# GLA values of two heads in one product of 512 columns, with the last gates and the first head's weight loads placed elsewhere

## The chip, the cores and the metric

The kernel runs on one core of a Trainium2 chip. The metric is the device time of one execution in microseconds (us), from the start of the program to its end. A core has five engines with their own instruction streams: PE (TensorE, the matmuls, with PEld for the weight loads), DVE (VectorE), ACT (ScalarE), POOL (GpSimd) and SP (SyncE), which issues most of the DMAs. Each engine executes its stream in order. Streams wait for one another through semaphores.

## The reference

One layer of a decoder on 2048 prompt tokens and 64 sample tokens (8 sequences of 8), with model width 1024. An input projection feeds two branches; the branches are merged by sigmoid gates, projected once more and normalized. The part that the change touches is the second branch, gated linear attention (GLA), with 4 heads of 128 keys and 256 values.

```python
z = jnp.einsum('btd,dn->btn', x, w_in)
q, k, v, g_att, gq, gk, gv, g_gla, g_lr, r_att, r_gla = jnp.split(z, SPLIT_POINTS, axis=-1)
...
def step(S, xs):                       # GLA, one chunk of tokens
    qc, kc, vc, gc = xs
    b = jnp.cumsum(gc, axis=1)
    b_last = b[:, -1]
    qt = qc * jnp.exp(b)
    kt = kc * jnp.exp(-b)
    kend = kc * jnp.exp(b_last[:, None] - b)
    o_inter = jnp.einsum('bthk,bhkv->bthv', qt, S)
    A = jnp.where(causal, jnp.einsum('bthk,bshk->bhts', qt, kt), 0.0)
    o_intra = jnp.einsum('bhts,bshv->bthv', A, vc)
    S = jnp.exp(b_last)[..., None] * S + jnp.einsum('bshk,bshv->bhkv', kend, vc)
    return S, o_inter + o_intra
...
o_gla = o_gla * lax.rsqrt(jnp.mean(jnp.square(o_gla), -1, keepdims=True) + EPS) * gla_norm_w
h_att = jnp.einsum('bta,ad->btd', o_att * jax.nn.silu(g_att), w_pa)
h_gla = jnp.einsum('btv,vd->btd', o_gla * jax.nn.silu(g_gla), w_pg)
merged = jax.nn.sigmoid(r_att) * h_att + jax.nn.sigmoid(r_gla) * h_gla
y = jnp.einsum('btd,de->bte', merged, w_o)
```

## The kernel before

Every dense product is made of three matmuls on values split in a high and a low part (fp32r): high by high, high by low, low by high. ACT casts the high part (L122) and DVE subtracts it from the value for the low part (L123). `proj` (L210 to L212) has weights stationary and tokens as columns; `proj_t` (L223 to L225) has the tokens stationary and the weights as columns, so its output has tokens on partitions.

The program has four stages. Attention runs from 0 to about 408 us: the 2112 tokens go in six chunks of 384, 384, 384, 384, 256 and 320 columns (`CHUNKS`), and in each the projections alternate with pieces of softmax work. GLA follows until about 1061 us: a loop over the 4 heads, in each the same six chunks. Then come four merge passes (L1268 to L1270), which use a Strassen-like recombination of blocks, and at last the output projection w_o with 512 columns per matmul (also L223 to L225).

In one GLA chunk the order on PE is written out by hand: the decay input (`gla_z`), values v for each block of 128 tokens (256 columns of one head), then k, q and two gate products g0 and g1. The recurrence of a chunk, the chain, runs through `at` and `tick`: `at(n, f)` puts f in a side list, and each `tick()` between products emits what is due. Its steps are `gla_a` (k by q for one block, masked by L763, and the key transpose), `gla_b` (output and state update, with the state split for the next block) and `gla_c` (the output's transpose, multiplied into the gate tile `sg` at L813). The chain of one chunk runs during the products of the next. In the last chunk of head 3 it runs during its own gates (`mid` puts a tick inside a product), and the sample tokens follow (`samp_a`, `samp_b`).

The order on the other engines comes from the framework's scheduler, which emits each engine's work as its operands become due; their streams are then fixed. Activations x are stored split in DRAM (`xs_d`) and loaded per chunk on SP; the gate input `gin` is loaded on POOL's queue. Finished gate tiles are stored to `ug_d` on SP, in the last chunk of head 3 on POOL. Three kinds of side work are threaded in: weight loads (`wload`, tile wst, cast to wh at L122 and wl at L123, up to a limit set by `wcap`), combinations of blocks for the merge passes (`combine_load` at L886, sums at L892 to L895, stores at L897), and in the last attention chunk the first head's weights. In that chunk `step` calls `wload` after every product, and `keys` writes kT (L611) after the key splits (L368 to L374).

Of the kernel before, what the change touches and what calls it, by code (L numbers as in the profile page):

```python
# [12 lines left out]
F32 = mybir.dt.float32  # L13
# [8 lines left out]
P = 128  # L22
# [28 lines left out]
def xwide(c):  # L51


    return 2 * CHUNKS[c][1] + (NS if c == len(CHUNKS) - 1 else 0)
# [3 lines left out]
def kernel(ctx, tc, io):  # L58
# [13 lines left out]
    def pd():  # L72
        return psd.tile([P, 512], F32, tag="pd", name="pd")
# [4 lines left out]
    def wtile(dt=F32, name="w"):  # L78
        return sb.tile([P, D], dt, tag="w", name=name, bufs=25)
# [16 lines left out]
    ac_d = dram.tile([4, P, MS, 2, MT], F32, name="ac_d")  # L96
    uc_d = dram.tile([4, P, MS, KT // 2, MT], F32, name="uc_d")
    xs_d = [dram.tile([4, P, 2 * xwide(c)], F32, name=f"xs{c}_d") for c in range(len(CHUNKS))]
    gl_d = dram.tile([96, NT], F32, name="gl_d")
    bs_d = dram.tile([NH, P, LB], F32, name="bs_d")  # L100

# [3 lines left out]
    def at(d, fn):  # L105

        while len(side) <= d:
            side.append([])
        side[d].append(fn)
# [34 lines left out]
    def wget():  # L144
        if not wready:
            wload()
        return wready.popleft()
# [173 lines left out]
    def setup1():  # L321


        oh, rbh, rbl, ssel, scol = (st1[n] for n in ("oh", "rbh", "rbl", "ssel", "scol"))
        for h in range(0, NH, 2):
            brow = wtile(name="brow")[:, :2 * LB].rearrange("p (h j) -> p h j", h=2)
            for j in range(2):
                bps = pa()
                mm(bps[:, :LB], rbh[:, h + j], oh, start=True, stop=False)
                mm(bps[:, :LB], rbl[:, h + j], oh, start=False, stop=True)  # L330
                if j:
# [3 lines left out]
            nc.sync.dma_start(bs_d[h:h + 2].rearrange("h q j -> q h j"), brow)  # L335
# [225 lines left out]
    def wcap(n):  # L561
        wseq[1] = n
# [18 lines left out]
    for c, (t0, T) in enumerate(CHUNKS):  # L581
# [13 lines left out]
        def step(ps_use, w=None):  # L595
            if w is not None:
                ps = pd()
                proj(ps[:, :T], w, x, T)
                ps_use(ps[:, :T])
            if last:  # L600
                wload()
            tick()

        if last:
            gin = gate_in(0, 0)

# [95 lines left out]
    def rot(key):  # L702
        r = R[key][cnt[key] % len(R[key])]
        cnt[key] += 1
        return r
# [63 lines left out]

    def gla_norm(B, key, o, n):  # L770

        on = rot("on")
        sq = small([P, 1], "sq")
        nc.scalar.activation(on[:n], o, AF.Square, scale=1.0 / 16, accum_out=sq[:n])  # L774
        nc.gpsimd.tensor_scalar(sq[:n], sq[:n], EPS, None, op0=ALU.add)  # L775
        nc.gpsimd.tensor_tensor(sq[:n], sq[:n], mhalf[:n], ALU.pow)
        nc.scalar.mul(on[:n], o, sq[:n])
        B["on", key] = on
# [35 lines left out]

    def gla_store(B):
        for m in range(2):
            (nc.gpsimd if B["last"] and B["h"] == GH - 1 else nc.sync).dma_start(
                ug_d[B["h"]][:, m, B["t0"]:B["t0"] + B["T"]], B["sg"][m][:, :B["T"]])


# [78 lines left out]
    def chain(B):  # L899

        last, nt = B["last"], B["nt"]
        if B["h"] == 0 and B["t0"] == 0:
            rings()
        short = nt == 2 and not last
        for i in range(nt):
            at(i, lambda B=B, i=i: gla_a(B, i))
            at((3, 5)[i] if short else i + 2, lambda B=B, i=i: gla_b(B, i))
            at((6, 7)[i] if short else i + 4, lambda B=B, i=i: gla_c(B, i, P, i * P))
        if last:
            at(nt + 2, lambda B=B: (nc.gpsimd if B["h"] == GH - 1 else nc.sync).dma_start(  # L910
                io["o_sp"][B["h"]], R["S"][sstate[B["h"]]]))
            at(nt - 1, lambda B=B: samp_a(B))
            at(nt + 1, lambda B=B: samp_b(B, 0))
            at(nt + 2, lambda B=B: samp_b(B, 4))
            o = nt + 4 if B["h"] == GH - 1 else nt + 5
            at(o, lambda B=B: gla_c(B, "s", NS, B["Tp"]))
            at(o, lambda B=B: gla_store(B))
        else:
            at(7 if short else 6, lambda B=B: gla_store(B))

    for h in range(GH):
        W2 = {}
        wcap(16 + 6 * h)
        for c, (t0, T) in enumerate(CHUNKS):
            last = c == len(CHUNKS) - 1
            Tp = T - (NS if last else 0)
            nt = Tp // P
            if c == len(CHUNKS) - 3:
                wcap(min(22 + 6 * h, 34))
            B = dict(h=h, t0=t0, T=T, Tp=Tp, nt=nt, last=last, wgk=R["wgk"], gin=gin, gv=[], sg=[])  # L930

            def wt2(*key):
                if c == 0:
                    W2[key] = wget()
                return W2[key]

            gla_z(B)
# [7 lines left out]
            wv = [wt2("v", 0), wt2("v", 1)]  # L945
            for i in range((T + P - 1) // P):
                n = min(P, T - i * P)
                ps = pd()
                if n == P:
                    proj_t(ps[:, :HV], x, i * P, n, wv, HV)  # L950
                    v = ps[:, :HV]
                else:
                    v = unit(name="vs")[:n, :HV]
                    proj_s(ps[:, :HV], v, x, i * P, wv, HV)
                    nc.vector.tensor_tensor(v, v, ps[:n, :HV], ALU.add)
                if i % 2 == 0:
                    gvt = wtile(F32R, "gv").rearrange("p (a b v) -> p a b v", a=2, b=2)
                gh, gl = gvt[:, i % 2, 0], gvt[:, i % 2, 1]
                split(gh[:n], gl[:n], v)
                if n == NS:  # L960
                    nc.scalar.copy(gh[NS:], v)
                    nc.vector.tensor_tensor(gl[NS:], v, gh[:NS].bitcast(F32), ALU.subtract)
                B["gv"].append((gh, gl))
                if last and i < 2:
                    wload()
                tick()
            end = last and h == GH - 1
            if not end:
                xn = tiles(load_x((c + 1) % len(CHUNKS)))
            ps = pd()  # L970
            proj(ps[:, :T], wt2("k"), x, T)
            gla_k(B, ps[:, :T])
            combine()
            if len(CHUNKS) - 4 < c < len(CHUNKS) - 1:
                wload()
            tick()
            if not last:
                gin = gate_in(h, c + 1)
            elif h + 1 < GH:
                gin = gate_in(h + 1, 0)  # L980
            ps = pd()
            proj(ps[:, :T], wt2("q"), x, T)
            gla_q(B, ps[:, :T])
            tick()
            combine()
            if end:
                chain(B)
            for m in range(2):
                sg = unit(name="sg")
                B["sg"].append(sg)  # L990
                w = wt2("g", m)
                ps = pd()
                proj(ps[:, :T], w, x, T, mid=end)
                gate(sg, ps[:, :T], T)
                if len(CHUNKS) - 4 < c < len(CHUNKS) - 1 and m == 1:
                    wload()
                tick()
            if not end:
                chain(B)
            x = xn  # L1000


# [384 lines left out]
def _layout(i):  # L1387
# [20 lines left out]
    wo = a["w_o"][0]  # L1408
    t = [cm(k), cm(v)] + [cm(heads(q, g)) for g in range(G)] + [cm(heads(ga, g)) for g in range(G)]
    for h in range(GH):  # L1410
        vh = gv[:, h * HV:(h + 1) * HV].reshape(2, 4, P, HV).transpose(0, 2, 1, 3).reshape(2, P, D)
        t += [vh[0], vh[1], cm(gk[:, h * HK:(h + 1) * HK]), cm(gq[:, h * HK:(h + 1) * HK])]
        t += [cm(gg[:, h * HV + m * P:h * HV + (m + 1) * P]) for m in range(2)]
    t_o = [rows(wo[:, nh * 512:(nh + 1) * 512], k0) for nh in range(2) for k0 in range(0, KT, 2)]

    def blocks(m):
# [58 lines left out]
```

## Time and profile before

| what | value |
|---|---|
| median of 3 executions | 1863.12 us (1858.07, 1863.60, 1863.12) |
| profiled execution | 1860.13 us, span 1858.4 us |
| mean granted TensorE clock in it | 0.989 |
| busy in the span | DVE 1196.7 us, ACT 770.0 us, POOL 391.2 us |
| DMA traffic | 368.98 MB, mean 199 GB/s |

The page gives busy time by engine, the span in 40 slices, DMA queues, the chain of work that ended last, and the costliest groups of instructions, each with the idle time before it and what ended that. "L210 PE MATMUL pd<-x,wh 128*128 128x384" is line 210, writing pd from the operands x and wh. A bracket such as [7.89 <-ACT kT L611] after an instruction says that its engine stood idle 7.89 us, and that ACT's write of kT at line 611 ended that. A matmul's own duration contains the pipeline; the pace of a stream is read from start to start.

### The profile page before, as it was taken

The page shows a single profiled execution, that of the slowest core. Times are in us where ns is not written, and L with a number is a line of the kernel's source. Part 1 is how long each engine was busy: PE and PEld are TensorE (multiplying, and loading weights), DVE is VectorE, ACT ScalarE, POOL GpSimd, SP SyncE. Part 2 cuts the span into 40 slices and gives each one's busy share as a digit, 9 for nine tenths or more (in the row PEclk, how much of TensorE's full clock was granted, in tenths as well). Part 3 has the DMA queues.
Part 4 walks back from the last instruction along what each step waited for, and adds up shares of the span by engine and source line. Part 5 has one row for each costly group of instructions (what it writes and reads, how often), then busy time and mean ns, then how long its engine had stood idle before and what let it go on. Part 6 is the DMA issues. An engine that isn't in the chain of part 4 may idle for free.

```text
span 1858.4 us, 31579 instructions
## 1 busy us (share of the span) xinstructions
PE 1809.5 (97%) x11683; PEld 1721.9 (93%) x11683; DVE 1196.7 (64%) x2470; ACT 770.0 (41%) x1735; POOL 391.2 (21%) x511
## 2 busy tenths in 40 slices
PE   7999999999999999999999989999999999989997
PEld 6998998889999999999999989999999999977886
DVE  5676777556665565566555559658657566966655
ACT  4444444443553454445444443445454543211110
POOL 2400000201011011011010124420355253631111
PEclk8999999999999999999999989999999999999999
DMA  7621234355565555745655089858887967895531
GB/s 263 234 81 63 74 107 162 121 181 191 195 223 177 211 213 177 256 145 191 220 204 177 29 262 322 277 192 284 278 319 261 307 217 245 283 300 188 161 114 40
DMA packets 188858, 368.98 MB, mean 199 GB/s; under 512 B 19981, under 2 KB 135141, under 8 KB 188688
## 3 DMA queue, kind: packets, MB, share of 16 engines
q1 hardware_dynamic: 181936, 357.82, 56.4%
q0 software_dynamic: 5616, 7.58, 1.4%
q8 instruction: 92, 1.51, 0.3%
q10 hardware_dynamic: 1152, 1.57, 0.3%
q14 instruction: 62, 0.51, 0.1%
HBM read 264.17 MB, written 103.70 MB: 198 GB/s over the span
## 4 chain that ended last, share of the span: by engine, by line
PE 86%; DMA 6%; DVE 4%; issue 1%; ACT 1%; POOL 1%; SPq 0%; DVEq 0%; POOLq 0%; ACTq 0%
PE pd L210 11%; PE pd L211 10%; PE pd L212 10%; PE pa L1269 8%; PE pa L1268 8%; PE pa L1270 8%; PE pd L225 6%; PE pd L223 6%; PE pd L224 6%; DMA wst<-wt 2%; DMA cs<-tt_d 2%; PE pa L449 1%; PE pa L434 1%; PE pa L783 1%; PE pa L784 1%
## 5 line engine op out<-in xcount | busy, mean ns | idle before, releaser
L210 PE MATMUL pd<-x,wh 128*128 128x384 f32 (+2 forms) x1248 | 411.1, 329 | 13.2 <-ACT kT L611 7.9
L212 PE MATMUL pd<-x,wl 128*128 128x384 f32 (+2 forms) x1248 | 404.7, 324 | 1.1 <-DVE wl L123 1.1
L211 PE MATMUL pd<-x,wh 128*128 128x384 f32 (+2 forms) x1248 | 405.2, 325 | 0.0
L1269 PE MATMUL pa<-xl,wh 128*128 128x352 f32 x1176 | 380.4, 323 | 8.6 <-DVE xl L123 8.0
L1268 PE MATMUL pa<-xh,wh 128*128 128x352 f32 x1176 | 382.1, 325 | 6.7 <-ACT wh L122 4.4
L1270 PE MATMUL pa<-xh,wl 128*128 128x352 f32 x1176 | 378.9, 322 | 0.0
L210 PEld LDWEIGHTS pd<-x,wh 128*128 128x128 f32 x1248 | 237.7, 190 | 24.0 <-issue 8.9
L212 PEld LDWEIGHTS pd<-x,wl 128*128 128x128 f32 x1248 | 237.4, 190 | 1.7 <-DVE wl L123 1.7
L211 PEld LDWEIGHTS pd<-x,wh 128*128 128x128 f32 x1248 | 237.8, 191 | 1.3 <-DVE x L123 1.2
L1269 PEld LDWEIGHTS pa<-xl,wh 128*128 128x128 f32 x1176 | 222.9, 190 | 12.0 <-DVE xl L123 11.9
L1268 PEld LDWEIGHTS pa<-xh,wh 128*128 128x128 f32 x1176 | 222.2, 189 | 8.6 <-ACT wh L122 5.0
L1270 PEld LDWEIGHTS pa<-xh,wl 128*128 128x128 f32 x1176 | 222.2, 189 | 0.0
L123 DVE TENSOR_TENSOR xl<-xs,xh 128x1408 fp32r<-128x1408 f32 x63 | 111.3, 1766 | 71.0 <-ACT xh L122 70.8
L223 PE MATMUL pd<-wh,x 128*128 128x256 f32 x512 | 147.9, 289 | 0.0
L224 PE MATMUL pd<-wh,x 128*128 128x256 f32 x512 | 144.7, 283 | 0.0
L225 PE MATMUL pd<-wl,x 128*128 128x256 f32 x512 | 144.7, 283 | 0.0
L775 POOL TENSOR_SCALAR sq<-sq 128x1 f32<-128x1 f32 (+1 forms) x68 | 18.6, 274 | 566.1 <-ACT ring L774 566.0
L122 ACT CAST xh<-xs 128x1408 fp32r<-128x1408 f32 x63 | 86.5, 1373 | 106.8 <-PE pa L1270 83.9
L225 PE MATMUL pd<-wol,x 128*128 128x512 f32 x256 | 101.6, 397 | 0.5 <-DVE wol L123 0.5
L123 DVE TENSOR_TENSOR wl<-ws,wh 128x512 fp32r<-128x512 f32 (+1 forms) x112 | 86.9, 787 | 23.2 <-ACT wh L122 22.6
L223 PE MATMUL pd<-woh,x 128*128 128x512 f32 x256 | 101.6, 397 | 0.0
L224 PE MATMUL pd<-woh,x 128*128 128x512 f32 x256 | 101.5, 396 | 0.0
(317 smaller groups left out, 3455.6 us busy)
## 6 DMA issues: line engine op xcount, KB each, us to landing
x<-xs_d SPq DMA_DIRECT2D x64, 768.0 KB, 6.4
wst<-wt SPq DMA_DIRECT2D x33, 512.0 KB, 3.8
xs<-xc_d SPq DMA_DIRECT2D x24, 704.0 KB, 5.7
cs<-tt_d SPq DMA_DIRECT2D x48, 352.0 KB, 4.9
xs<-xT SPq DMA_DIRECT2D x18, 704.0 KB, 6.5
xs_d<-x SPq DMA_DIRECT2D x16, 768.0 KB, 5.3
x<-xs_d SPq DMA_DIRECT2D x16, 704.0 KB, 5.9
ws<-w_ra SPq DMA_DIRECT2D x36, 256.0 KB, 4.6
```

What stands on the lines that cost most here:

```text
L122: pin["a"] = nc.scalar.copy(dst_h, src)
L123: i = eng.tensor_tensor(dst_l, src, dst_h.bitcast(F32), ALU.subtract)
L210: mm(ps, hi[:, s], xh[:, :T], start=(k == 0), stop=False)
L211: mm(ps, hi[:, s], xl[:, :T], start=False, stop=False)
L212: mm(ps, lo[:, s], xh[:, :T], start=False, stop=(k == n - 1))
L223: mm(ps, xh[:, xs], hi, start=(k == 0), stop=False)
L224: mm(ps, xl[:, xs], hi, start=False, stop=False)
L225: mm(ps, xh[:, xs], lo, start=False, stop=(k == KT - 1))
L775: nc.gpsimd.tensor_scalar(sq[:n], sq[:n], EPS, None, op0=ALU.add)
L1268: mm(ps, wh[:, ks], xh[:, ts], start=(k == 0), stop=False)
L1269: mm(ps, wh[:, ks], xl[:, ts], start=False, stop=False)
L1270: mm(ps, wl[:, ks], xh[:, ts], start=False, stop=(k == q.kh - 1))
```

## The change

In even heads the value product covers the head and the next one: `values` uses four weight tiles of 512 columns, and the odd head's half, split, is stored to DRAM (`v_d`). The odd head loads it back (`load_v`). In odd heads the gates come first, with a tick in their middle, then k and q; the chain of the chunk before is shifted by one tick. At the start of k in each chunk, x, gin and (for odd heads) the values of the next chunk are requested (`ahead`). Combine sums run one per chunk from the second chunk on in tiles of their own (`stile`), and one more in two chunks of odd heads. In head 3, chunk 4 emits no gates: its normalized outputs stay in a tile `keep`, and after the last chunk's gates come the two gate products of chunk 4, its `gla_c` steps, and its store, on POOL. In the last attention chunk `wload` is called from the fourth step on. The bias rows of the setup (`brow`) are produced four heads at a time.

```diff
@@ setup
-        for h in range(0, NH, 2):
-            brow = wtile(name="brow")[:, :2 * LB].rearrange("p (h j) -> p h j", h=2)
-            for j in range(2):
+        for h in range(0, NH, 4):
+            brow = xslot(F32, "brow").rearrange("p (h j) -> p h j", h=4)
+            for j in range(4):
...
@@ attention, step
-            if last:
+            steps[0] += 1
+            if last and steps[0] > 3:
                 wload()
...
@@ gla_norm, gla_store
-        on = rot("on")
+        on = B["keep"][:, key * HV:(key + 1) * HV] if "keep" in B else rot("on")
...
-            (nc.gpsimd if B["last"] and B["h"] == GH - 1 else nc.sync).dma_start(
+            (nc.gpsimd if B["h"] == GH - 1 and B["c"] >= LAST - 1 else nc.sync).dma_start(
...
+    def values(B, i):
+        n = min(P, B["T"] - i * P)
+        ps = pd()
+        if n == P:
+            proj_t(ps, x, i * P, n, wv, 512)
+            v = ps
...
+        for j, t in enumerate(B["gvt"]):
+            gh, gl = t[:, i % 2, 0], t[:, i % 2, 1]
+            vj = v[:n, j * HV:(j + 1) * HV]
+            split(gh[:n], gl[:n], vj)
...
+            elif i % 2 or (i + 1) * P >= B["T"]:
+                m = (i % 2 + 1) * 512
+                nc.sync.dma_start(v_d[B["h"] // 2][B["c"]][i // 2, :, :m],
+                                  t.rearrange("p a b v -> p (a b v)")[:, :m].bitcast(F32))
...
+    def load_v(h, c):
...
+            t = wtile(F32R, "gv")
+            nc.sync.dma_start(t[:, :m * 512].bitcast(F32), v_d[h // 2][c][i // 2, :, :m * 512])
...
-            sums = [combine_load(lambda n: wtile(name=n)) for _ in range(2 if c in (1, 2, 3) else 0)]
+            sums = [combine_load(stile)] if c else []
+            if odd and c in (1, 2):
+                sums.append(combine_load(lambda n: wtile(name=n)))
...
+            xn, gin, gvn = ahead()
+            if odd and not end:
...
+                for m in range(2):
+                    gates(B, x, m, True)
...
+            if h == GH - 1 and LAST - 2 <= c < LAST:
+                Bn = chunk(h, c + 1, gin, gvn)
+            dense(B, x, wt2("k"), gla_k, odd)
...
+            if end and not last:
+                B["keep"] = wtile(name="keep")
+                chain(B, 1, late=True)
+                Bg, xg = B, x
+            elif end:
                 chain(B)
+                for m in range(2):
+                    gates(B, x, m, True)
+                for m in range(2):
+                    gates(Bg, xg, m, True)
+                for i in range(Bg["nt"]):
+                    gla_c(Bg, i, P, i * P)
+                drain()
+                gla_store(Bg)
```

Three places in the streams. The first is ACT in the last attention chunk, before the change; pT is the copy of the transposed probabilities, wst the loaded weights and wh their high part, kd the key splits.

```order
L418 ACTIVATE s,sm<-s,nm 128x256 x4
L420 ACTIVATE es<-es 128x4
L122 CAST wh<-wst 128x1024 x2
L438 COPY pT<-pa 128x512
L122 CAST wh<-wst 128x1024
L368 CAST kd_3454<-pd 64x256
L369 CAST kd_3455<-pd 64x256
L373 CAST kd_3454<-pd 64x256
L374 CAST kd_3455<-pd 64x256
L611 COPY kT<-pd 128x320
```

After the change two of the three weight casts are gone from there (the lines below 600 shift by one, the kT line by three).

```order
L419 ACTIVATE s,sm<-s,nm 128x256 x4
L421 ACTIVATE es<-es 128x4
L439 COPY pT<-pa 128x512
L123 CAST wh<-wst 128x1024
L369 CAST kd_3462<-pd 64x256
L370 CAST kd_3463<-pd 64x256
L374 CAST kd_3462<-pd 64x256
L375 CAST kd_3463<-pd 64x256
L614 COPY kT<-pd 128x320
```

The second place is DVE at the end of head 3, where a sum of blocks (x) stands beside the chain (aper is the masked k by q, ak its split, ring the state) and the key products (em, ek). Before:

```order
L763 COPY_PREDICATED aper_170<-cmask,pa 128x128
L123 TENSOR_TENSOR st<-ring,st 128x256
L123 TENSOR_TENSOR ak<-aper_170,ak 128x128
L123 TENSOR_TENSOR ak<-pa,ak 128x128
L892 TENSOR_TENSOR x_11393<-x_11393,x_11392 128x352
L893 TENSOR_TENSOR x_11392<-x_11392 128x352
L894 TENSOR_TENSOR x_11392<-x_11392,x_11393 128x352
L895 TENSOR_TENSOR x_11393<-x_11392,x_11393 128x352
L748 TENSOR_TENSOR em<-pd,em 128x384
```

And after, in head 3's chunk 4:

```order
L895 TENSOR_TENSOR x_11084<-x_11084,x_11083 128x352
L896 TENSOR_TENSOR x_11083<-x_11083 128x352
L751 TENSOR_TENSOR em<-pd,em 128x256
L742 COPY e_11123<-gb 128x2
L745 COPY e_11125<-gb 128x8
L751 TENSOR_TENSOR ek<-pd,ek 128x256
L897 TENSOR_TENSOR x_11083<-x_11083,x_11084 128x352
L766 COPY_PREDICATED aper_180<-cmask,pa 128x128
L898 TENSOR_TENSOR x_11084<-x_11083,x_11084 128x352
L124 TENSOR_TENSOR ak<-aper_180,ak 128x128
L124 TENSOR_TENSOR ak<-pa,ak 128x128
```

The sum now stands ahead of the mask and the splits. Its loads stand on SP (after) behind the store of the sum before and an x load between them:

```order
L195 DMA x<-xs_d 128x1408
L900 DMA uc_d<-x_10826 128x2x352
L900 DMA uc_d<-x_10827 128x2x352
L195 DMA x<-xs_d 128x1408
L889 DMA x_11083<-ug_d 128x704
L889 DMA x_11084<-ug_d 128x704
L195 DMA x<-xs_d 128x1408 x2
```

The third place is the end of GLA. On SP before, the last stores of gate tiles (chunk 4 is 128x256) stand ahead of the first loads of the merge passes, xc and ws:

```order
L817 DMA ug_d<-sg 128x384 x2
L817 DMA ug_d<-sg 128x256 x2
L1073 DMA xc<-ua_d 128x2x352
L1042 DMA ws<-w_pa 128x256 x4
```

After, chunk 4's stores have left SP:

```order
L848 DMA S_11480<-state 128x4x256
L848 DMA S_11482<-state 128x4x256
L820 DMA ug_d<-sg 128x384 x2
L1143 DMA xc<-ua_d 128x2x352
L1112 DMA ws<-w_pa 128x256 x4
```

They are on POOL now, behind those of the last chunk; the xc load takes memory that the gate tiles held, and waits for these stores:

```order
L874 DMA o_ss<-S_11480 128x4x256
L778 TENSOR_SCALAR sq<-sq 64x1
L779 TENSOR_TENSOR sq<-sq,mhalf 64x1
L874 DMA o_ss<-S_11482 128x4x256
L820 DMA ug_d<-sg 128x320 x2
L820 DMA ug_d<-sg 128x256 x2
```

More of the change, by code (lines that the diff above doesn't have):

```diff
@@ L98 @@
     xs_d = [dram.tile([4, P, 2 * xwide(c)], F32, name=f"xs{c}_d") for c in range(len(CHUNKS))]
+    v_d = [[dram.tile([2, P, D], F32, name=f"v{p}{c}_d") for c in range(len(CHUNKS))] for p in range(GH // 2)]
     gl_d = dram.tile([96, NT], F32, name="gl_d")
@@ L330, in setup1 @@
                 mm(bps[:, :LB], rbl[:, h + j], oh, start=False, stop=True)
-                if j:
+                if j % 2:
                     nc.vector.tensor_copy(brow[:, j], bps[:, :LB])
@@ L334, in setup1 @@
                     nc.scalar.copy(brow[:, j], bps[:, :LB])
-            nc.sync.dma_start(bs_d[h:h + 2].rearrange("h q j -> q h j"), brow)
+            nc.sync.dma_start(bs_d[h:h + 4].rearrange("h q j -> q h j"), brow)
         sps = pa()
@@ L599, in step @@
                 ps_use(ps[:, :T])
-            if last:
+            steps[0] += 1
+            if last and steps[0] > 3:
                 wload()
             tick()
+        steps = [0]
         if last:
@@ L897, in combine_do, with chain @@
             nc.sync.dma_start(dst[n_:n_ + 2].rearrange("n p t -> p n t"), x_.rearrange("p (n t) -> p n t", n=2))
-    def chain(B):
+    def chain(B, o=0, late=False):
         last, nt = B["last"], B["nt"]
@@ L903, in chain @@
             rings()
-        short = nt == 2 and not last
+        short = nt == 2 and not last and o == 0
+        end = last and B["h"] == GH - 1
         for i in range(nt):
-            at(i, lambda B=B, i=i: gla_a(B, i))
-            at((3, 5)[i] if short else i + 2, lambda B=B, i=i: gla_b(B, i))
-            at((6, 7)[i] if short else i + 4, lambda B=B, i=i: gla_c(B, i, P, i * P))
+            at(o + i, lambda B=B, i=i: gla_a(B, i))
+            at((3, 5)[i] if short else o + i + 2, lambda B=B, i=i: gla_b(B, i))
+            if not late:
+                at((6, 7)[i] if short else o + i + 4, lambda B=B, i=i: gla_c(B, i, P, i * P))
@@ L909, in chain @@
         if last:
-            at(nt + 2, lambda B=B: (nc.gpsimd if B["h"] == GH - 1 else nc.sync).dma_start(
+            at(o + nt + 2, lambda B=B: (nc.gpsimd if end else nc.sync).dma_start(
                 io["o_sp"][B["h"]], R["S"][sstate[B["h"]]]))
[L912 to L916, printed above, removed]
@@ L917, in chain @@
-            at(o, lambda B=B: gla_store(B))
-        else:
-            at(7 if short else 6, lambda B=B: gla_store(B))
+            at(o + nt - 1, lambda B=B: samp_a(B))
+            at(o + nt + 1, lambda B=B: samp_b(B, 0))
+            at(o + nt + 2, lambda B=B: samp_b(B, 4))
+            at(o + nt + 5, lambda B=B: gla_c(B, "s", NS, B["Tp"]))
+            at(o + nt + 5, lambda B=B: gla_store(B))
+        elif not late:
+            at(7 if short else o + nt + 4 if o else 6, lambda B=B: gla_store(B))
@@ new lines, in values @@
+    def values(B, i):
[4 more added lines that the diff above has]
+            v = ps
+        else:
+            v = wtile(name="vs")[:n, :512]
+            proj_s(ps, v, x, i * P, wv, 512)
+            nc.vector.tensor_tensor(v, v, ps[:n], ALU.add)
+        if i % 2 == 0:
+            B["gvt"] = [wtile(F32R, nm).rearrange("p (a b v) -> p a b v", a=2, b=2) for nm in ("gv", "gvo")]
+        for j, t in enumerate(B["gvt"]):
+            gh, gl = t[:, i % 2, 0], t[:, i % 2, 1]
+            vj = v[:n, j * HV:(j + 1) * HV]
+            split(gh[:n], gl[:n], vj)
+            if n == NS:
+                nc.scalar.copy(gh[NS:], vj)
+                nc.vector.tensor_tensor(gl[NS:], vj, gh[:NS].bitcast(F32), ALU.subtract)
+            if j == 0:
+                B["gv"].append((gh, gl))
+            elif i % 2 or (i + 1) * P >= B["T"]:
+                m = (i % 2 + 1) * 512
+                nc.sync.dma_start(v_d[B["h"] // 2][B["c"]][i // 2, :, :m],
+                                  t.rearrange("p a b v -> p (a b v)")[:, :m].bitcast(F32))
@@ new lines, in load_v, with chunk @@
+    def load_v(h, c):
+        out = []
+        n = (CHUNKS[c][1] + P - 1) // P
+        for i in range(0, n, 2):
+            m = min(2, n - i)
+            t = wtile(F32R, "gv")
+            nc.sync.dma_start(t[:, :m * 512].bitcast(F32), v_d[h // 2][c][i // 2, :, :m * 512])
+            t = t.rearrange("p (a b v) -> p a b v", a=2, b=2)
+            out += [(t[:, j, 0], t[:, j, 1]) for j in range(m)]
+        return out
+    LAST = len(CHUNKS) - 1
+    def chunk(h, c, gin, gv):
+        t0, T = CHUNKS[c]
+        last = c == LAST
+        Tp = T - (NS if last else 0)
+        B = dict(h=h, c=c, t0=t0, T=T, Tp=Tp, nt=Tp // P, last=last, wgk=R["wgk"], gin=gin, gv=gv, sg=[])
+        gla_z(B)
+        return B
@@ L921, with dense, gates, wt2 @@
+    def dense(B, x, w, use, mid):
+        ps = pd()
+        proj(ps[:, :B["T"]], w, x, B["T"], mid=mid)
+        use(B, ps[:, :B["T"]])
+    def gates(B, x, m, mid):
+        sg = unit(name="sg")
+        B["sg"].append(sg)
+        dense(B, x, wt2("g", m), lambda B, ps: gate(sg, ps, B["T"]), mid)
+        tick()
     for h in range(GH):
         W2 = {}
[L923 to L937, printed above, removed]
-            sums = [combine_load(lambda n: wtile(name=n)) for _ in range(2 if c in (1, 2, 3) else 0)]
+        odd = h % 2
+        def wt2(*key):
+            if key not in W2:
+                W2[key] = wget()
+            return W2[key]
+        for c in range(len(CHUNKS)):
+            last = c == LAST
+            end = h == GH - 1 and c >= LAST - 1
+            if not end:
+                B = chunk(h, c, gin, gvn if odd else [])
+            else:
+                B = Bn
+            sums = [combine_load(stile)] if c else []
+            if odd and c in (1, 2):
+                sums.append(combine_load(lambda n: wtile(name=n)))
@@ L943, in combine @@
                         combine_do(*sums.pop(0), nc.vector)
[L945 to L964, printed above, removed]
-                    wload()
-                tick()
@@ L967, with ahead @@
[L967 to L972, printed above, removed]
+            def ahead():
+                nh, nx = (h, c + 1) if not last else (h + 1, 0)
+                if nh == GH:
+                    return None, None, None
+                return tiles(load_x(nx)), gate_in(nh, nx), load_v(nh, nx) if nh % 2 else []
+            if not odd:
+                wv = [wt2("v", i) for i in range(4)]
+                if c == 0:
+                    wcap(wseq[0] + 2)
+                for i in range((B["T"] + P - 1) // P):
+                    values(B, i)
+                    if c == 0:
+                        wload()
+                    tick()
+                if last:
+                    wcap(wseq[0] + 4)
+                    wload(2)
@@ L973 @@
+            xn, gin, gvn = ahead()
+            if odd and not end:
+                if h < GH - 1 and c == 2:
+                    wcap(wseq[0] + 6)
+                for m in range(2):
+                    gates(B, x, m, True)
+                    if last:
+                        wload()
+                if 1 < c:
+                    wload()
+            if h == GH - 1 and LAST - 2 <= c < LAST:
+                Bn = chunk(h, c + 1, gin, gvn)
+            dense(B, x, wt2("k"), gla_k, odd)
             combine()
-            if len(CHUNKS) - 4 < c < len(CHUNKS) - 1:
+            if not odd and last:
@@ L975 @@
                 wload()
             tick()
[L977 to L983, printed above, removed]
+            dense(B, x, wt2("q"), gla_q, odd)
+            if not odd and last:
+                wload()
             tick()
             combine()
-            if end:
-                chain(B)
[L988 to L997, printed above, removed]
@@ L998 @@
-            if not end:
-                chain(B)
+            if end and not last:
[3 more added lines that the diff above has]
+            elif end:
+                chain(B)
+                for m in range(2):
[6 more added lines that the diff above has]
+                gla_store(Bg)
+            else:
+                if not odd:
+                    for m in range(2):
+                        gates(B, x, m, False)
+                chain(B, 1 if (h if not last else h + 1) % 2 else 0)
@@ L1410, in _layout @@
     for h in range(GH):
-        vh = gv[:, h * HV:(h + 1) * HV].reshape(2, 4, P, HV).transpose(0, 2, 1, 3).reshape(2, P, D)
-        t += [vh[0], vh[1], cm(gk[:, h * HK:(h + 1) * HK]), cm(gq[:, h * HK:(h + 1) * HK])]
-        t += [cm(gg[:, h * HV + m * P:h * HV + (m + 1) * P]) for m in range(2)]
+        kq = [cm(gk[:, h * HK:(h + 1) * HK]), cm(gq[:, h * HK:(h + 1) * HK])]
+        gs = [cm(gg[:, h * HV + m * P:h * HV + (m + 1) * P]) for m in range(2)]
+        t += gs + kq if h % 2 else [rows(gv[:, h * HV:(h + 2) * HV], k0) for k0 in range(0, KT, 2)] + kq + gs
     t_o = [rows(wo[:, nh * 512:(nh + 1) * 512], k0) for nh in range(2) for k0 in range(0, KT, 2)]
```

## The prediction

> **What bounds the kernel now.** I read the page's busy shares first.
>
> ```profile
> span 1858.4 us, 31579 instructions
> PE 1809.5 (97%) x11683; PEld 1721.9 (93%) x11683; DVE 1196.7 (64%) x2470; ACT 770.0 (41%) x1735; POOL 391.2 (21%) x511
> PE   7999999999999999999999989999999999989997
> ```
>
> TensorE is busy 97% of the span, so only about 49 us are without matmul work, and the 40 slices put them at the start, at slice 23, near slice 36 and at the end. Next comes the list of what PE waited for.
>
> ```profile
> PE pa L1269 <- DVE xl L123: 8.0, 5, 2.1
> PE pd L210 <- ACT kT L611: 7.9, 1, 7.9
> PE pa L1268 <- ACT wh L122: 4.4, 2, 4.1
> ```
>
> One stall of 7.9 us (kT, the end of attention) and several at the start of the merge passes stand out. Then the stages, by windows (columns: PE, PEld, DVE, ACT, POOL busy, granted clock, DMA share, GB/s).
>
> ```profile
> 408.00:1061.00 653.00, 653.00 (x4747) 646.43 (x4745) 384.75 (x1016) 304.31 (x756) 72.79 (x160) 1.00 0.54 189
> 1300.00:1480.00 180.00, 180.00 (x1135) 180.00 (x1134) 114.24 (x151) 86.02 (x136) 74.92 (x57) 1.00 0.83 290
> 610.00:615.00 5.00, 5.00 (x45) 5.00 (x44) 3.58 (x9) 3.23 (x7) 0.00 (x0) 1.00 1.03 410
> ```
>
> The GLA loop, 408 to 1061, is PE from end to end at full clock. Its time is its matmul time, and there is slack everywhere else: DVE 59%, ACT 47%, DMA 54%. Two things follow. The change can gain there only by fewer or shorter matmul steps, and it can lose there as soon as something else, now hidden, arrives late. All sums are made against the profiled execution, 1860.13 us (span 1858.4); the median of three runs is 1863.12, so that execution is 3.0 us on the fast side. A measurement of this kernel tells about 0.3%, 5.6 us, from no change.
>
> **The 512 columns.** The removed matmuls are the values' 256-column ones, three lines of 512 each; the 512-column kind exists already, in the last stage.
>
> ```profile
> L223 PE MATMUL pd<-wh,x 128*128 128x256 f32 x512 | 147.9, 289 | 0.0
> ```
> ```profile
> 639.88 0.28 PE L225 MATMUL pd<-wl,x 128*128 128x256 f32 x1
> 640.00 0.28 PE L223 MATMUL pd<-wh,x 128*128 128x256 f32 x1
> ...
> 1700.23 0.40 PE L223 MATMUL pd<-woh,x 128*128 128x512 f32 x1
> 1700.47 0.39 PE L224 MATMUL pd<-woh,x 128*128 128x512 f32 x1
> ```
>
> A row's own duration (0.28, 0.40) includes the pipeline; what counts is start to start: 0.120 us at 256 columns, and 0.234 at 512 (ten starts from 1699.76 to 1701.87). 1536 x 0.120 = 184.3 us become 768 x 0.234 = 179.7: **-4.6 us**. Both ends: nothing, if the weight load (0.19 us a piece) were already the pace at either width, and -6. The weight loads halve too, but they overlap. The rows measured stand in for the new ones exactly, so I take -4.6. By the Trainium skill's TensorE: Matmul & The Clock Gate, section Back-to-back issue gap, an isolated matmul takes N/2.4 + 2.5 ns, so a pair of 256 costs only about 2.5 ns more than one of 512 and the sum here would be an estimated -2 us. The trace has 6 ns per pair; the rows decide.
>
> **The first head's weight loads, later.** Before, ACT casts weights in the last attention chunk amid the work that PE waits for.
>
> ```profile
> 320.80 0.58 ACT L438 COPY pT<-pa 128x512 f32<-128x512 f32 x1
> 323.58 1.05 ACT L122 CAST wh<-wst 128x1024 fp32r<-128x1024 f32 x1 [2.21 <-DMA wst<-wt]
> 324.54 0.36 ACT L368 CAST kd<-pd 64x256 fp32r<-64x256 f32 x1
> 327.58 0.36 ACT L373 CAST kd<-pd 64x256 fp32r<-64x256 f32 x1 [2.30 <-DVE kl L372]
> 328.36 0.42 ACT L611 COPY kT<-pd 128x320 f32<-128x320 f32 x1
> ```
> ```profile
> 319.92 1.04 PE L434 MATMUL pa<-ident,s 128*128 128x128 f32 x8
> 328.84 0.64 PE L210 MATMUL pd<-x,wh 128*128 128x320 f32 x1 [7.89 <-ACT kT L611]
> ```
>
> PE ends its transposes at 320.96 and waits for kT until 328.84. ACT could go on at 321.38, but the next cast in its order has no data until 323.58. The new order has one cast there, of weights loaded long before, and then the same kd, kd, kd, kd, kT. So the 2.21 us of DMA wait goes; the cast (1.05), the kd casts and the wait for kl on DVE stay: these are late next. DVE's wl split behind the late cast moves up with it. kT then ends near 326.5 instead of 328.8: **-2.3 us**. Bounds: 0 (kl sets the time regardless) and -7.9 (everything gone). I stay near the 2.21, because that is the only piece whose cause is removed. The loads moved behind step 4 fall in a stretch where PE has products to do.
>
> **Odd heads: a new order, and values read back.** Odd heads do no value products; their values come from DRAM. The work that DVE, ACT and the queues do per chunk shrinks little, but a chunk of 384 columns falls from about 30 us of PE to about 21 us. Hence the density rises: my count of each chunk's DVE operations at their durations gives 0.78 to 0.91 of PE's time in odd heads, against 0.66 at most before. A DVE with that little slack serves its queue in order, and late. Two places come out with no cover, from the order and these rows:
>
> ```profile
> L892 DVE TENSOR_TENSOR x<-x,x 128x352 f32<-128x352 f32 x24 | 12.4, 517 | 0.1
> L748 DVE TENSOR_TENSOR em<-pd,em 128x384 f32<-128x384 f32 x16 | 8.8, 552 | 7.1 <-PE pd L212 7.1
> L763 DVE COPY_PREDICATED aper<-cmask,pa 128x128 f32<-128x128 uint32 x64 | 18.9, 296 | 4.7 <-PE pa L761 2.7
> ```
> ```profile
> x<-xs_d SPq DMA_DIRECT2D x64, 768.0 KB, 6.4
> ...
> x<-ug_d SPq DMA_DIRECT2D x12, 352.0 KB, 5.4
> uc_d<-x SPq DMA_DIRECT2D x12, 352.0 KB, 2.7
> xc<-ac_d SPq DMA_DIRECT2D x12, 352.0 KB, 4.4
> ```
>
> First, **the end of head 3**. The combine sums (L892 to L895 before, L895 to L898 after) now have two buffers of their own. The next sum's load waits for the previous sum's store: 0.4 to issue, 2.7 to land, 0.8 for two issues, 5.4 to land = 9.3 us. In the new order that store stands on SP behind an x load that waits for PE to finish a product, and the sum's four operations stand on DVE ahead of the masks (L763) and splits of the next chain step. Counted from the release of the x load to the splits: 9.3 + 4 x 0.52 + about 1.3 for the masks, multiplications and splits between = 12.7 us, and PE has 10.3 us of work to do before it needs them: 2.4 us of stall. The next sum, built the same way, costs a further 1.5. **+4.0 us**; from 0 (loads land in 3 us) to +8 (both in full, 2 x 4).
>
> Second, **the last chunk of head 1**: q's product takes the PSUM bank of k's, which is freed by two multiplications (L748, about 0.5 each at 320 columns) standing behind two sums of 0.52 and smaller work: 1.0 + 0.8 = **+1.8 us**, from 0 to +3. Gates-first elsewhere, the gate inputs and x loaded at a chunk's start: I cost them at nothing, since x is issued 19 us or more before its use in head 1 and lands in about 6. Where that cover is gone (the last chunk of head 3, 11 us ahead) it just fits. The setup's brow in fours: the same PE work and the same order, 0 within 0.5.
>
> The extra traffic is 17.5 MB, most of it in heads 1 and 3. By my count head 1 moves 40.8 MB in 120.7 us of PE work, 338 GB/s. 290 GB/s took a share of 0.83, so the whole would be 349; 5 us ran at 410. It fits barely, chunk 1 of head 1 above it. **+1.5 us**, from 0 to +8: the worst chunk asks 374 against 349, 21 us x 0.07.
>
> **The tail.** Before, the chain's end runs bare on PE:
>
> ```profile
> 1062.20 0.34 ACT th L245
> 1062.56 0.49 DVE sg L246
> ...
> 1072.22 0.55 POOL ug_d L817
> 1072.77 3.04 DMA ug_d<-sg
> 1075.84 0.35 issue
> 1076.27 2.18 DMA ws<-w_pa
> 1078.48 0.41 ACT wh L122
> ```
> ```profile
> 1062.87 0.38 PE L782 MATMUL pa<-st,qih 128*128 128x256 f32 x1 [0.89 <-ACT st L122]
> ...
> 1070.10 0.70 PE L810 MATMUL pa<-ident,ring 128*128 128x128 f32 x4 [1.01 <-ACT ring L777]
> 1071.07 0.43 PE L1268 MATMUL pa<-xh,wh 128*128 128x352 f32 x1 [0.27 <-ACT wh L122]
> ...
> 1078.93 0.66 PE L1268 MATMUL pa<-xh,wh 128*128 128x352 f32 x1 [4.13 <-ACT wh L122]
> ...
> 1082.62 0.35 PE L1268 MATMUL pa<-xh,wh 128*128 128x352 f32 x1
> ```
>
> From 1071.07 to 1082.62 there are 18 matmuls of 0.160 at full speed, 2.9 us, in 11.55: 8.7 lost, of which about 1.6 is a half clock after the gap (0.29 start to start). With the ring wait (1.2), the gap before 1071.07 (0.5) and the st waits (1.5): 11.9 lost. The change covers the ring wait. But in the new order the first merge load on SP, xc, reuses the memory of the last gates and waits for their stores, which come at the very end; before, the first xc and ws were loaded ahead, so six merge matmuls could start at 1071.07. From the last gate matmul: gate 0.34 + 0.49, five ring multiplications and latencies 1.3, two store issues 0.55, landing 3.04, issue 0.4, xc 4.4 (3.1 at best), and its casts 0.4 and more: 10.6 us, less 0.5 for transposes. With 1.7 half clock and the same st waits: 13.4. **+1.5 us**, from 0 to +5. The same page of the Trainium skill (Part 1: The HAM clock gate) has the clock halve when PE idles a few us; the 0.29 us after a gap of 4 us agree.
>
> **Sum**: -4.6 - 2.3 + 4.0 + 1.8 + 1.5 + 1.5 = +1.9: 1860.1 + 1.9 = **1862.0 us**, within 0.3% of before.
>
> **Rivals.** A, *slower: the odd heads are fed too slowly*. One mechanism: in heads 1 and 3 DMA and DVE queues run full, every sum's load lands late, and the in-order DVE hands that on to the chain. It decides once the real rate under this mix falls below 338 GB/s. At 320, between the 290 measured and the 349 it stands for, head 1 takes 127.5 us instead of 120.7, +6.8, and half of that in head 3: +10 in place of the 1.5, 1871. For it: DVE near 0.9, a share of 0.83 at just 290. Against it: 410 GB/s for 5 us. The Trainium skill's DMA: Bandwidth & Descriptors, section Specifications, gives about 358 GB/s from HBM per core; by it head 1 needs an estimated 114 us, under PE's 120.7, so it speaks against A.
>
> B, *faster: the stalls do not come*. The gains stand alone: 1860.1 - 4.6 - 2.3, with the tail even and small waits for other loads, **1853**; with all of kT's wait 1848. For it: PE waited for nothing in the whole loop before; against it, two dependencies that I can count.
>
> C, *the parts do not do what they say*: kT stays behind kl as before and the tail's cover goes to waits: 1860.1 - 4.6 + 8.8 = 1864, within the same bound.
>
> **How the numbers follow.** Forecast and C, 0.52 (own range 1857 to 1868); A 0.26; B 0.22. Range 1851 to 1873: it reaches into both rivals up to the kT bound's middle and A's price. Slower by over 0.3% is A, 0.26; faster B, 0.22; the same 0.52.
>
> **What would show it.** Start to start of 0.234 in the values of heads 0 and 2; kT's wait near 5.6; PE waits inside the loop, for the splits ak behind L895 at the end of head 3 (2 to 4 us) and for L751 in the last chunk of head 1; a gap of about 10 us before the first merge matmul. No PE wait in the loop means B; waits in many chunks of heads 1 and 3, with a DMA share near 1, mean A.

## The result, and the profile after

The changed kernel takes 1869.01 us (median of 8 executions, 1865.38 to 1872.03), the one before 1863.36 us (8 executions). The ratio is 1.0032, with a 95% interval of 1.0017 to 1.0046. On the chip of the first experiments it was 1.0045 (1.0029 to 1.0061). So the change makes the kernel a little slower: some 6 to 8 us, about the smallest step that can be told here. The profiled execution of the changed kernel took 1869.35 us.

The list of what PE waited for, in the changed kernel (columns: engine and line, releaser, us in total, times, longest):

```profile
PE pa L1339 <- DVE xl L124: 8.4, 5, 3.3
PE pa L1338 <- ACT wh L123: 7.7, 1, 7.7
PE pd L211 <- ACT kT L614: 5.3, 1, 5.3
...
PE pd L718 <- DMA gin<-gl_d: 4.4, 1, 4.4
PE pa L785 <- ACT st L123: 2.5, 5, 0.9
PE pd L211 <- DVE ek L751: 2.3, 1, 2.3
PE pa L813 <- ACT ring L780: 1.5, 1, 1.5
PE pa L785 <- ACT ak L123: 1.4, 1, 1.4
```

Before, the loop had no wait at all until its very end. Now gin, st, ek, ring and ak stand in it. The stages show where they are, by windows of the changed kernel: head 1, head 3, and the two even heads.

```profile
582.00:712.00 130.00, 126.74 (x842) 122.16 (x841) 93.87 (x250) 73.75 (x178) 21.21 (x42) 1.00 0.90 309
928.00:1060.00 132.00, 123.34 (x803) 118.39 (x802) 89.93 (x258) 68.57 (x177) 20.27 (x41) 0.97 0.73 254
361.00:582.00 221.00, 221.00 (x1372) 199.80 (x1371) 114.73 (x296) 94.44 (x236) 17.79 (x37) 1.00 0.48 166
712.00:927.00 215.00, 215.00 (x1241) 196.29 (x1240) 108.36 (x276) 88.02 (x216) 19.14 (x41) 1.00 0.50 176
```

The windows' columns are again PE, PEld, DVE, ACT and POOL busy, granted clock, DMA share and GB/s. PE is full in the even heads, idle for 3.3 us in head 1 and for 8.7 us in head 3, where the mean granted clock is 0.97. Head 1 has DMA at a share of 0.90 with 309 GB/s, DVE at 72% (93.87 of 130). From the first gate input's matmul to the 19th matmul of the merge passes (the stretch used below to compare traces), the profiled execution takes 726.3 us against 717.3 before: +9.0 us, in spite of the cheaper value products.

### The profile page after: what moved, and what is told of

The parts are those of the page before. It is cut to its first block, busy times and chain, and to the rows that moved or that the text cites. A ratio compares the mean times of both kernels' runs of the same rounds, so it can differ in the third digit from the quotient of the medians.

```text
span 1867.6 us, 30009 instructions
## 1 busy us (share of the span) xinstructions
PE 1810.2 (97%) x10883; PEld 1686.4 (90%) x10883; DVE 1198.0 (64%) x2468; ACT 770.2 (41%) x1733; POOL 394.4 (21%) x513
## 4 chain that ended last, share of the span: by engine, by line
PE 85%; DMA 5%; DVE 4%; ACT 1%; issue 1%; POOL 1%; SPq 0%; DVEq 0%; POOLq 0%; ACTq 0%
PE pd L211 10%; PE pd L213 10%; PE pd L212 10%; PE pa L1339 8%; PE pa L1340 8%; PE pa L1338 8%; PE pd L226 6%; PE pd L224 6%; PE pd L225 6%; DMA cs<-tt_d 2%; PE pa L450 2%; PE pa L435 1%; PE pa L786 1%; PE pa L787 1%; PE pa L785 1%
## 5 line engine op out<-in xcount | busy, mean ns | idle before, releaser
L224 PE MATMUL pd<-wh,x 128*128 128x512 f32 x256 | 101.7, 397 | 0.0
L226 PE MATMUL pd<-wl,x 128*128 128x512 f32 x256 | 99.9, 390 | 0.0
L225 PE MATMUL pd<-wh,x 128*128 128x512 f32 x256 | 99.9, 390 | 0.0
L123 ACT CAST x<-xst 128x384 fp32r<-128x384 f32 (+5 forms) x68 | 38.2, 569 | 148.9 <-PE pd L225 117.3
```

Source lines behind the costliest of these rows:

```text
L123: pin["a"] = nc.scalar.copy(dst_h, src)
L224: mm(ps, xh[:, xs], hi, start=(k == 0), stop=False)
L225: mm(ps, xl[:, xs], hi, start=False, stop=False)
L226: mm(ps, xh[:, xs], lo, start=False, stop=(k == KT - 1))
```

## The experiments

Three theories stood against one another. **W**: the loss is a handful of new PE waits inside the GLA loop, each with a place. **P**: the merge passes run at a slower pace because of the change. **D**: DVE and DMA queues are full in odd heads, and waits only move when one is taken away.

**The changed kernel once more**, without an edit.

> The changed kernel, unaltered, for a second profile. Theory W (new waits inside the GLA loop make the loss): the same waits come again at the same places: gin 4.4 us, ek L751 2.3 us, ak 1.4 us, ring 1.5 us, and the time is 1.002 to 1.005 of before. Rival P (the merge passes run at a slower pace because of the change): the start to start there is again 161.1 ns, not 158.9, from about 1150 to 1540 us. If the pace is a matter of the single execution, it may come out as 158.9 this time, and the time of the profiled execution then is about 5 us less.

The waits came again: wh 7.9, kT 5.3, gin 4.4, st 2.5, ek 1.8, ring 1.5, ak 1.1; the ratio is 1.0045. The GLA loop is repeatable: from the first gate input's matmul to the first merge matmul it takes 721.4 and 721.3 us in the two profiles. The pace of the merge passes was another. And **the kernel before once more**:

> The kernel before, unaltered, for a second profile. If the pace of the merge passes is a matter of the single execution, it can be 158.9 or 161.1 ns here as well; the waits are those of the first profile (kT 7.9, wh 4.1, xl 8.0) within 1 us.

The number of matmuls in the same 280 us of the merge passes gives the pace; the four lines are before, before again, after and after again.

```profile
1200.00:1480.00 280.00, 280.00 (x1765) 280.00 (x1764) 184.96 (x265) 132.99 (x210) 91.64 (x71) 1.00 0.80 273
```
```profile
1200.00:1480.00 280.00, 280.00 (x1740) 280.00 (x1739) 182.94 (x263) 131.05 (x207) 92.23 (x71) 1.00 0.79 270
```
```profile
1200.00:1480.00 280.00, 280.00 (x1740) 280.00 (x1739) 185.99 (x264) 130.72 (x206) 95.31 (x73) 1.00 0.80 270
```
```profile
1200.00:1480.00 280.00, 280.00 (x1764) 280.00 (x1763) 186.26 (x266) 131.85 (x209) 100.67 (x75) 1.00 0.81 274
```

1765 and 1740 matmuls in 280 us are 158.6 and 160.9 ns each. Both kernels have both paces, so P falls: the pace belongs to the execution. It is worth 5 us (the profiled executions of the kernel before took 1860.13 and 1865.71 us), and the first two profiles had drawn opposite ones. From the 19th merge matmul to the first of the output projection they take 574.6 us before and 578.1 after, so 3.5 of the 9.2 us between these two profiles lie behind the changed part.

**The later weight loads alone**, in the kernel before.

```diff
+            steps[0] += 1
-            if last:
+            if last and steps[0] > 3:
                 wload()
...
+        steps = [0]
```

> The kernel before with only the first head's weight loads started at step 4 of the last attention chunk. W: the kT wait falls from 7.9 to about 5.4 us and nothing else changes: -2.5 us, ratio 0.9987. Rival: a stall reappears in the first GLA chunk, because the weights come later; then the ratio is 1.000.

The ratio is 0.9985 (0.997 to 1.0), 1859.01 us against 1861.57. The wait is as expected, and no other came:

```profile
PE pd L210 <- ACT kT L613: 5.3, 1, 5.3
```

**The gate input of head 3's last chunk, issued earlier.** The changed kernel shows how it comes late. On POOL (timeline: start, duration, instruction, idle before):

```profile
1013.08 0.66 POOL L778 TENSOR_SCALAR sq<-sq 128x1 f32<-128x1 f32 x1 [3.65 <-ACT ring L777]
1013.82 0.74 POOL L779 TENSOR_TENSOR sq<-sq,mhalf 128x1 f32<-128x1 f32 x1
1018.17 0.52 POOL L778 TENSOR_SCALAR sq<-sq 128x1 f32<-128x1 f32 x1 [3.61 <-ACT ring L777]
1018.77 0.95 POOL L779 TENSOR_TENSOR sq<-sq,mhalf 128x1 f32<-128x1 f32 x1
1019.68 0.59 POOL L577 DMA_DIRECT2D gin<-gl_d  x1
```

POOL itself is idle most of that time. The load stands behind the normalization of the chain's last block, which waits for ACT; it leaves at 1019.68, takes 5.4 us, and PE, which needs it at 1020.7, waits until 1025.09. The clock is halved behind the gap (0.50 in the next 2 us):

```profile
1025.09 0.64 PE L718 MATMUL pd<-gin,wgk 96*128 96x320 f32 x1 [4.37 <-DMA gin<-gl_d]
```
```profile
1025.00:1027.00 2.00, 1.91 (x8) 1.91 (x9) 0.55 (x1) 1.19 (x3) 0.00 (x0) 0.50 1.05 413
```

Until 1028.30 the 256-column matmuls start 0.214 us apart instead of 0.120, which costs a further 1.4 us. In the edit, `early` keeps a gate input that was requested one chunk ahead.

```diff
-                return tiles(load_x(nx)), gate_in(nh, nx), load_v(nh, nx) if nh % 2 else []
+                xs_, g = tiles(load_x(nx)), early.pop() if early else gate_in(nh, nx)
+                if nh == GH - 1 and nx == LAST - 1:
+                    early.append(gate_in(nh, LAST))
+                return xs_, g, load_v(nh, nx) if nh % 2 else []
```

> Only the load of the gate input for head 3's last chunk is issued about 25 us earlier, next to that of chunk 4. W: the PE wait for gin (4.4 us plus 0.3 of half clock) is gone, the ak wait behind it grows from 1.4 to about 2.4 since the sum's load no longer has that time: net -3.5 us, ratio to before near 1.001. Rival D (the loop is limited by full DVE and DMA queues in odd heads, the waits only move): the time stays at 1.003 and other waits in head 3 take the place.

1863.84 us, ratio 1.0017 (1.0005 to 1.0028), 5.4 us less than the changed kernel on the same chip. The gin wait is gone. The ak wait grew to 3.1 us, and by the lines below it isn't a sum on DVE that makes it. ACT in this run, and then PE:

```profile
1025.53 0.47 ACT L723 ACTIVATE ga<-ga 128x320 f32<-128x320 f32 x1
1028.03 1.28 ACT L737 ACT_TABLE_LOAD   x1 [2.03 <-DVE dm L730]
1029.32 0.47 ACT L737 ACTIVATE em<-dm 128x320 f32<-128x320 f32 x1
1029.70 0.45 ACT L738 ACTIVATE ek<-ek 128x320 f32<-128x320 f32 x1
```

```profile
1031.27 0.39 PE L785 MATMUL pa<-gv,ak 128*128 128x256 f32 x1 [3.10 <-ACT ak L123]
```

The exponentials of the last chunk, which the change prepares one chunk ahead, stand on ACT before the casts of ak, and wait themselves for DVE. DVE had made the masks by 1029.2 us; the first cast of ak starts at 1030.78, behind the last exponential. In the changed kernel, too, DVE first waits for these exponentials, and only one of the sum's four operations (L897, 0.51 us) then stands ahead of the mask:

```profile
1033.28 0.17 DVE L742 COPY e<-gb 128x2 f32<-128x2 f32 x1 [1.11 <-ACT gb L740]
1033.36 0.16 DVE L745 COPY e<-gb 128x8 f32<-128x8 f32 x1
1033.43 0.42 DVE L751 TENSOR_TENSOR ek<-pd,ek 128x256 f32<-128x256 f32 x1
1033.77 0.51 DVE L897 TENSOR_TENSOR x<-x,x 128x352 f32<-128x352 f32 x1
1034.20 0.29 DVE L766 COPY_PREDICATED aper<-cmask,pa 128x128 f32<-128x128 uint32 x1
```

**Without the deferred gates.** Chunk 4 of head 3 keeps its gates, and its store goes back to SP; the rest of the change stays.

```diff
-            (nc.gpsimd if B["h"] == GH - 1 and B["c"] >= LAST - 1 else nc.sync).dma_start(
+            (nc.gpsimd if B["h"] == GH - 1 and B["c"] == LAST else nc.sync).dma_start(
...
-            end = h == GH - 1 and c >= LAST - 1
+            end = h == GH - 1 and c == LAST
...
-            if h == GH - 1 and LAST - 2 <= c < LAST:
-                Bn = chunk(h, c + 1, gin, gvn)
...
-            if end and not last:
-                B["keep"] = wtile(name="keep")
-                chain(B, 1, late=True)
-                Bg, xg = B, x
-            elif end:
+            if end:
                 chain(B)
                 for m in range(2):
                     gates(B, x, m, True)
-                for m in range(2):
-                    gates(Bg, xg, m, True)
-                for i in range(Bg["nt"]):
-                    gla_c(Bg, i, P, i * P)
                 drain()
-                gla_store(Bg)
...
-                chain(B, 1 if (h if not last else h + 1) % 2 else 0)
+                chain(B, 1 if (h if not last else h + 1) % 2 and not (h == GH - 1 and c == LAST - 1) else 0)
```

> Head 3's chunk 4 keeps its gates and the last chunk is laid out as before the change; paired values, odd heads' order and the later weight loads stay. W: gin 4.4, ring 1.5, ak 1.4 and the st waits of head 3's end (1.5) go, the tail is as before the change: about -8 us against the changed kernel, ratio to before 0.998 to 0.999. D: the waits show up elsewhere in heads 1 and 3 and the ratio stays above 1.001.

1856.12 us against 1861.57 before and 1869.21 for the changed kernel on that chip: ratio 0.9967 (0.9952 to 0.9982). That is 13 us less than the changed kernel, where 8 were expected. The waits for gin and ak are gone. What was not expected is the end of GLA, on SP. In the kernel before, and then here:

```profile
1063.47 0.37 SPq L1073 DMA_DIRECT2D xc<-ua_d  x1
1064.03 13.56 SPq L1042 DMA_DIRECT2D ws<-w_pa  x4
```
```profile
1064.03 1.81 SPq L1099 DMA_DIRECT2D ws<-w_pa  x4
1065.94 0.94 SPq L1130 DMA_DIRECT2D xc<-ua_d  x2
1066.97 0.90 SPq L1099 DMA_DIRECT2D ws<-w_pa  x2
```

Before, the four ws loads took 13.56 us to issue: the second waited for the last store of gate tiles to land, and the others stood behind it. Here the first load that waits for that store is the tenth, six ws loads leave by 1068, and the 4.1 us wait for wh in the merge passes' start is absent. A weight load needs nothing of that store but the memory, so the tiles must lie elsewhere; the placement was not tried apart. In the changed kernel xc itself waits, and leaves at 1078.20, after the stores that chunk 4's late gates bring:

```profile
1076.10 1.07 POOL L820 DMA_DIRECT2D ug_d<-sg  x2 [0.20 <-DVE sg L816]
```
```profile
1078.20 0.37 SPq L1143 DMA_DIRECT2D xc<-ua_d  x1
```

**Two products of 256 columns instead of one of 512**, in the changed kernel, with the same loads and stores.

```diff
-            proj_t(ps, x, i * P, n, wv, 512)
+            for j in range(2):
+                cs = slice(j * HV, (j + 1) * HV)
+                proj_t(ps[:, cs], x, i * P, n, wv, 512, cs)
```

> The changed kernel, but each value product of 512 columns is made as two of 256, in the same PSUM bank, from the same weight tiles and with the same stores and loads. By the forecast's rows (0.120 and 0.234 us) it is 4.6 us slower than the changed kernel; by the mean of all value matmuls in the two traces (0.1218 before, 0.2304 after) 1536 x 0.1218 - 768 x 0.2304 = 10.1 us slower, ratio to before about 1.009 against 1.004.

1877.78 us, ratio 1.0086 (1.0071 to 1.0101) against 1.0032 and 1.0045 of the changed kernel: 0.0041 to 0.0054 of 1861.5, 8 to 10 us. In the traces the stretch from the first gate input's matmul to the 19th merge matmul is 735.7 us, 9.3 more than in the changed kernel. Of the two values expected, 4.6 and 10.1, the larger is the nearer. A whole product shows why, first and last of 24 starts, before and after:

```profile
641.34 0.36 PE L223 MATMUL pd<-wh,x 128*128 128x256 f32 x1
...
644.16 0.28 PE L225 MATMUL pd<-wl,x 128*128 128x256 f32 x1
```
```profile
361.28 0.40 PE L224 MATMUL pd<-wh,x 128*128 128x512 f32 x1
...
366.51 0.40 PE L226 MATMUL pd<-wl,x 128*128 128x512 f32 x1
```

23 intervals in 2.82 and 5.23 us are 0.1226 and 0.2274 us, not the 0.120 of the middle of a product and the 0.234 of the output projection. The second is the fastest product of its kind: the mean is 0.2302 over all 32 after, and 0.1218 over all 64 before. In values_256 itself the mean at 256 columns is 0.1209, and 1536 x 0.1209 - 768 x 0.2302 = 8.9 us, as measured.

**Three sums left to the merge passes**, once with the early gate input (gin_nosum) and once without the deferral (no_end_nosum). Head 1's last chunk and head 3's last two make no combine sum; POOL makes them in the third merge pass, beside the six that it makes anyway.

```diff
+            late = (h == 1 and c == LAST) or (h == GH - 1 and c >= LAST - 1)
-            sums = [combine_load(stile)] if c else []
+            sums = [combine_load(stile)] if c and not late else []
```

> The early gate input, and three combine sums (head 1's last chunk, head 3's last two) left to the merge passes, where POOL does six already. W: the ek L751 wait (2.0 us) and the ak wait (3.1 us) go, because no sum stands ahead of those instructions on DVE: about -5 us against gin_early, ratio to before 0.9985 to 0.999. Rival D (DVE is full in odd heads, whatever stands in its queue): at least half of both waits stays, ratio 1.001 or more. If POOL's three added sums are late for the third merge pass, a wait shows there instead.

> Chunk 4 keeps its gates (as no_end), and the same three sums are left to the merge passes. W: against no_end the ek L751 wait (2.0) goes; the st waits at 943 and 1060 (1.4 and 1.6) may shrink: -2 to -3 us, ratio to before 0.995. D: no difference to no_end.

Both got slower than the kernels that they start from (gin_early and no_end): 1874.18 us, ratio 1.0065 (1.0047 to 1.0082), and 1865.22 us, ratio 1.0019 (1.0006 to 1.0033). Inside the loop W was right about ek: that wait is gone in both, and without the deferral the loop is 6.3 us shorter than in no_end. It was wrong about ak, which stays at 3.1 us in gin_nosum, as the ACT lines above explain. The loss lies in the merge passes, where POOL's sums now come late: the last of nine starts at 1512.3 us in gin_nosum, the last of six at 1438.7 in gin_early. PE waited in gin_nosum for:

```profile
PE pa L1343 <- ACT xh L123: 6.5, 2, 6.1
...
PE pa L1343 <- DVE fin L1178: 3.2, 2, 2.8
PE pa L785 <- ACT ak L123: 3.1, 1, 3.1
```

**The three sums earlier in the loop**, without the deferral: chunks 1 and 2 of head 2 and chunk 3 of head 3 take them.

```diff
             sums = [combine_load(stile)] if c and not late else []
-            if odd and c in (1, 2):
+            if h and c in (1, 2) or h == GH - 1 and c == 3:
                 sums.append(combine_load(lambda n: wtile(name=n)))
```

> As no_end, but the three combine sums of head 1's last chunk and head 3's last two chunks are made earlier in the GLA loop (chunks 1 and 2 of head 2, chunk 3 of head 3), not in the merge passes. W: the GLA part is as in no_end_nosum (6 us shorter than in no_end), the merge passes as in no_end: ratio to before 0.993 to 0.995. D (odd heads' or chunk 3's queues are full): waits appear in the chunks that take the sums and the ratio is as no_end's, 0.997.

1850.53 us against 1861.19, ratio 0.9937 (0.9924 to 0.9950): faster than both kernels. The stretch to the 19th merge matmul is 708.8 us, against 713.1 in no_end and 717.3 before. Waits in the chunks that take the sums did not come, which speaks against D. So does head 1 in this run, where PE idles 0.8 of 127 us with the DMA share at 0.91:

```profile
581.00:708.00 127.00, 126.20 (x845) 122.34 (x844) 92.62 (x247) 74.63 (x180) 21.80 (x44) 1.00 0.91 318
```

## Why the prediction was partly right and where it failed

The forecast was no change, 1862.0 us within 1851 to 1873. The time lies in that range, but the move is real, and slower. That it lies there is partly luck: the value products gained 4 to 5 us more than forecast, which hid a part of what the loop lost. The forecast named several of the places of the loss, but for the costliest, the end of head 3, it had the wrong cause.

- **The 512 columns.** The mechanism was right, the size was not: the term of -4.6 should have been about -9 (8 to 10 by values_256). Two prices were taken at the wrong spot: the middle of a product for 256 columns (0.120, where whole products average 0.1218), and another stage for 512 (0.234, where the value products average 0.2302).
- **The weight loads of the first head.** -2.3 forecast, -2.6 measured (7.9 to 5.3), -2.6 us by the medians of kt_only, whose interval reaches to no change. kl and the kd casts were late next, as said.
- **The end of head 3.** This is the step that failed. It was put at +4.0, for sums late behind SP's stores and ahead of the splits on DVE, while gin was costed at nothing, with its load 11 us ahead of its use. The load left 1.0 us ahead (1019.68 against 1020.7), held by POOL's queue, and some 5 us are gin's (gin_early). The ak wait, put down to the sums, is 1.4 us, not 4, and waits for ACT's exponentials; in gin_nosum it stays without the sums. The whole deferral costs 13 us (no_end). In the traces these are gin 4.4 and the half clock behind it 1.4, ak 1.4, ring 1.5, and 4.6 at the end of GLA, where no_end also gains on the kernel before. Of these only gin was undone by itself.
- **The last chunk of head 1.** +1.8 forecast, 1.7 to 2.3 measured in the five profiles with that sum, and absent in the three runs without it. Beside the sums, the low part of wgk stands ahead on DVE too, after 0.8 us of waiting for ACT; it was not tried apart.
- **DMA crowding** was given +1.5. Head 1 ran at 309 GB/s, below the 338 that its planned work asked for, since the span was longer; PE waited there for no DMA but 0.2 to 0.7 us for the state. DVE was busy 72% of head 1 (65 to 83% by chunk), where the forecast counted 78 to 91%. Rival A, as a matter of rate, did not come, though the time went its way: in no_end_moved the same stretch runs at 318 GB/s almost without a wait.
- **The tail.** +1.5 forecast; the terms listed for its 10.6 us add up to 10.9. From the last start ahead of the st wait to the 19th merge matmul it takes 26.85 us after the change, of which 48 gate matmuls of 0.12 are 5.8: 21.1 us, against 20.95 before. The longer wait for xc and the cover of the ring wait cancelled. What the forecast didn't see is that some 4.5 us could be had there: in no_end the same stretch takes 16.5 us, because the first merge loads do not wait for the last stores.
- **Rivals B and C** did not come. B's condition, no stalls in the loop, is nearly that of no_end_moved, which came to 1850.53 us, near B's 1853.

With the wider columns at -9, kT at -2.6 and the loop's waits at +11 (gin 4.4, ek 2.3, ring 1.5, ak 1.4, and st 1.6 more than before) and 1.4 for the half clock behind gin, the sum is about +1, not the +6 measured. Of the remaining 5 us or so the trace shows about half: in odd heads the products of k, q and gates are cut in the middle for a chain step, and in the 384-column products the mean start to start within a product rose from 175.7 to 177.4 ns, 2.5 us over some 1440 intervals. Most of that (1.8 us) is one longer interval behind each of 28 cuts. No run isolates it, and the other half stays open.

## What to carry to other kernels

A load that a stage needs at once should not stand on a queue whose next instruction waits for another engine; read what is ahead of it there, not how far ahead it was written. When work is put later to fill a tail, look at what the tail's memory blocks: here the stores of the late gates held back the next stage's first loads. Price a matmul stream by the mean of many whole products in its own stage, first start to last, including the breaks; a single product can be the fastest of them.

## What the runs showed that was not expected

The merge passes run at one of two paces, 158.6 or 160.9 ns per matmul of 352 columns, with a granted clock of 1.00 in both. The pace can change after a stall and then stays until a later one; in the changed kernel's first profile it was the slower from about 1160 to 1540 us and the faster from 1550 on. Each of two kernels shows both paces in two profiles, so a single pair of profiles can differ by 5 us for no reason of the code. What sets it was not found.
